# Plain gate-up sets with tokens as rows, and a higher rank for readings, sums, softmax and normalisation, in a decoder layer on one Trainium2 core

## The chip, the cores and the metric

The kernel runs on one core of a Trainium2 chip, as one launch. The time is that of the whole kernel on the device, in microseconds; it stands beside a median of three runs. The engines are named as in the profile: PE (TensorE, matmuls), PEld (its weight loads), DVE (VectorE), ACT (ScalarE), POOL (GpSimd) and SP (SyncE, which here issues most of the loads).

## The reference

One layer of a decoder, for 512 tokens (T) of 2048 features (D), all in fp32. It has two token mixers side by side, joined by gates per channel, and a SwiGLU feed-forward part of width 5632 (DFF); the normalisations are scaled and shifted by vectors made from `c`.

```python
sh_a, sc_a, gt_a, sh_f, sc_f, gt_f = split(silu(c) @ w_ada + b_ada, 6)
h = rmsnorm(x, norm_mix) * (1.0 + sc_a) + sh_a
c_q, c_kv, k_pe, q_g, k_g, v_g, z, b_logit, a_logit, gate_logits = split_cols(h @ w_in)
y_a = mla_branch(c_q, c_kv, k_pe, ...) @ w_o_mla          # 8 heads, causal softmax over 512 keys
y_b = gdn_branch(conv_silu(q_g, k_g, v_g), z, b_logit, a_logit, ...) @ w_o_gdn   # gated delta rule
g_a, g_b = split(sigmoid(gate_logits), 2)
x = x + gt_a * ((g_a * y_a + g_b * y_b) @ w_o)
h = rmsnorm(x, norm_ffn) * (1.0 + sc_f) + sh_f
gate, up = split(h @ w_gate_up, 2)                         # 2 x 5632 columns
x = x + gt_f * ((silu(gate) * up) @ w_down)
return rmsnorm(x, final_norm)
```

(Written shorter than in the reference; the order and the shapes are the same.)

## The kernel before

Every fp32 operand of a matmul is split into two parts, `hi` (rounded to the matmul's format, a cast on ACT) and `lo` (the rest, a subtraction on DVE). A product is then three matmuls, hi with hi, hi with lo and lo with hi, that add up in the same bank of PSUM. Weights come by DMA and are split in the kernel: L263 is the cast to `hi`, L264 the subtraction for `lo` (`halves`); L239 and L240 do the same for activations (`hilo`).

**Units.** The work of TensorE is a list of *units*. A unit has a load (a DMA by SP), a split, a list of matmuls, and a step before and after them. For a plain weight matrix a unit is two row tiles of 128 by 512 columns. `Driver.run` takes the units in order, and keeps two of them split ahead (`AHEAD`) and up to four loaded. The parts split from weights stand in pools of four buffers each (`SPLITS`). Tiles of 128x512 for all else come from one pool of 68 (`SLOTS`). Matmuls write to 8 PSUM banks.

**Chains.** Side work (normalisation, sums, stores) is written as generators, *chains*. After every 12 matmuls counted (`GROUP`), each chain makes one step; `weight` says how much one matmul counts, and `hold` puts the next step off by 12.

**Order.** The instructions of PE, SP and POOL keep the order of the program (`PINNED`). DVE and ACT are ordered when the kernel is built, by a list scheduler: of the instructions that are ready the one with the lowest rank goes first, and the rank is the place in the program. `tc.high_priority(n)` takes n off the rank of what is issued inside it. Before the change, the work touched by it has its plain rank.

**Stages.** In order: the modulation vectors; the products with `w_in`, in sets of 512 columns; the delta rule and the attention in between; the two output products (`ya`, `yb`); the product with `w_o`, three quarters of it by a form of Strassen's method (`strassen`) and the last quarter, `wo3`, in two halves of 256 tokens (`half_sets`); the feed-forward part; its down product with the last normalisation.

**Around the change.** `wo_half_done` reads the banks of a half of `wo3`: it adds the gated result to the stream x2 (L1432), squares it on ACT, and adds up the squares (L1444). `part_rstd` sums the squares over the features with matmuls into a bank (`hss`), computes the reciprocal root with a row of small operations on DVE (`token_rstd`, `rsqrt`, L229 to L233 and L417) and makes a diagonal tile of it (L1467); `spread` broadcasts it over the rows with one matmul (`hbc`). `h2_gen` is the chain that then normalises the eight groups `q` of a token half `h` (two row tiles of 256 tokens each, L1752 and L1753), and splits each group for the matmuls. The chain of the first half starts in the second half of `wo3`, that of the second half in `gu0`.

The gate-up product takes 11 sets of 512 inner columns. The last ten (`big(1)` to `big(10)`) go by Strassen's method with tokens as the rows of the result; what they produce is turned by PE transposes in the second half of the set that follows (`turned_a`, which reads `turning`) and stored to `f_dram`, from where the down product reads it. The first 512 inner columns are two plain sets, `gu0` and `gu1`, of 256 gate and 256 up columns each: here the weights stand still and 256 tokens move, in two halves, so that the result has features as rows and needs no turning. `gu0` goes over all weights for one half of the tokens, then over all of them for the other half; `gu1` takes both halves with each weight tile. `gu_done` reads the banks at the end of a set: Silu of the gate on ACT, times the up part on DVE, stored from the tile `sl`.

`done` is the step that reads the banks of a set in general (`fm_set` for features as rows, `tm_set` for tokens as rows), `after` the same in the Strassen sets; `softmax`, `transposes` and `values` are the steps of the attention.

Of the kernel before, what the change touches and what calls it, by code (L numbers as in the profile page):

```python
# [11 lines left out]
AF = mybir.ActivationFunctionType  # L12
# [7 lines left out]
KT = 16  # L20
# [9 lines left out]
AHEAD = 2  # L30
LOADS = 4
GROUP = 12


class Unit:
# [136 lines left out]
def block_kernel(ctx: ExitStack, tc: tile.TileContext, a: dict, out, out_t):  # L172
# [34 lines left out]
    def tok(j):  # L207
        return slice(j * P, (j + 1) * P)

    def h4(ap):  # L210
        return ap.rearrange("p (h d) -> p h d", h=4)

# [67 lines left out]
    def fm_set(name, loads, width, kt, x, done, ks=None, lo_eng=None, st=None, small=False, cols=slice(0, T), alone=False, late=False,  # L280
               in_parts=()):
        widths = [min(P, width - o) for o in range(0, width, P)]
        st = {} if st is None else st

        def unit(k0, nk):
            box = {}

            def start():
                box["raw"] = fetch(loads(k0, nk), width, nk, small)

            def split():
                box["w"] = halves(box.pop("raw"), width, nk, nc.gpsimd if lo_eng and k0 % 4 == 0 else None, small)

            if in_parts and k0 == 0:
                def start():
                    raw = box["raw"] = raws.tile([P, nk, width], F32, tag="raw", name=nm("raw"))
                    for dst, src in loads(k0, nk):
                        for cs in in_parts:
                            load(dst(raw)[:, :, cs], src[:, :, cs])

                def split(between):
                    raw = box.pop("raw")
                    hi = his.tile([P, nk, width], F32R, tag="hi", name=nm("hi"))
                    lo = los.tile([P, nk, width], F32R, tag="lo", name=nm("lo"))
                    box["w"] = hi, lo
                    for i, cs in enumerate(in_parts):
                        nc.scalar.copy(hi[:, :, cs], raw[:, :, cs])
                        if i == 0:
                            between[0]()
                        nc.vector.tensor_tensor(lo[:, :, cs], raw[:, :, cs], hi[:, :, cs].bitcast(F32), ALU.subtract)  # L310
                        if i == 0:
                            between[1]()

            def pre():
                if k0 == 0 and cols.start == 0:
# [12 lines left out]

            def post():
                if k0 + nk == kt and done is not None:  # L330
                    done(st["ps"])
                    drv.hold()

            return Unit(start, split, mms, pre, post, alone=alone, late=late and k0 + nk == kt)

        return [unit(k0, nk) for k0, nk in ks or [(k, 2) for k in range(0, kt, 2)]]

    def tm_set(name, loads, kt, x, done, nk=2, ts=tuple(range(NT)), lo_eng=None, weight=1, alone=False, xt=None):
# [5 lines left out]
        def unit(k0):  # L344
# [21 lines left out]

            def post():
                if k0 + nk == kt:
                    done(st["ps"])
                    drv.hold()  # L370

            return Unit(start, split, mms, pre, post, weight=weight, alone=alone)
# [789 lines left out]
    def attention():  # L1162
# [5 lines left out]
        def scores(i):  # L1168
# [8 lines left out]
            if qb == 3:  # L1177
                del QN[h], KN[h], qpT[h]
                if h == 7:
                    kpT.clear()  # L1180

        def softmax(i):
            h, qb = items[i]
            N = (qb + 1) * P
# [8 lines left out]
            nc.vector.tensor_scalar(p[:, 0:N], p[:, 0:N], r, None, op0=ALU.mult)  # L1193
            box[i]["p"] = p

        def transposes(i):
            h, qb = items[i]
            N = (qb + 1) * P
            p = box[i].pop("p")
            ps = PS("pT")  # L1200
            for kb in range(qb + 1):
                nc.tensor.transpose(ps[:, tok(kb)], p[:, tok(kb)], ident)
            s = S("pT")
            (nc.scalar.copy if i % 2 else nc.vector.tensor_copy)(s[:, 0:N], ps[:, 0:N])
            box[i]["pT"] = s

        def values(i):
            h, qb = items[i]
            s = box[i].pop("pT")
# [228 lines left out]
    def squares(q, seg, eng):  # L1438
# [6 lines left out]
        else:  # L1445
            st.append(s)

    def part_rstd(segs):

        ps = PS("hss")  # L1450
# [37 lines left out]
    def half_sets(name, loads, x, done):  # L1488
# [3 lines left out]
        def unit(h, k0):  # L1492
# [20 lines left out]

            def post():
                if k0 + 2 == KT:
                    done(h, st[h])
                    st[h] = None
                    drv.hold()

# [220 lines left out]
    def start_h2(h):  # L1740
        return lambda: h2c.append(drv.add(h2_gen(h)))

    def h2_gen(h):

        yield 3 if h else 1
# [1 line left out]
        yield 6 if h else 4  # L1747
        r = spread(*diag)
        for q in range(8):
            f = S("h2f")  # L1750
            for k in (2 * q, 2 * q + 1):
                nc.vector.scalar_tensor_tensor(half_of(f, k), half_of(x2[h][q], k), s_ffn[:, k:k + 1], r, op0=ALU.mult, op1=ALU.mult)  # L1752
                nc.scalar.activation(half_of(f, k), half_of(f, k), AF.Identity, bias=sh_ffn[:, k:k + 1])  # L1753
            x2[h][q] = None
            h2f[h][q] = f
            h2T[h][q] = hilo(f[:], "h2")
            h2n[h] = 2 * q + 2
            yield 2

    w_gu, w_dn = a["w_gate_up"][0], a["w_down"][0]  # L1760
# [38 lines left out]
    def big(s):  # L1799
# [64 lines left out]
        def tt(o, x, y):  # L1864
            nc.vector.tensor_tensor(o, x, y[:], ALU.add)  # L1865

        def after(c, t):
            if c == "m1":
                nc.scalar.copy(v[t], ps["m1"][t][:])
# [126 lines left out]
    def strassen(w, c1, c0, products, ready, outputs, freed):  # L1996
# [6 lines left out]
        def unit(k):  # L2003
# [28 lines left out]

            res = {}

            def after(c):
                def tt(name, x, y, op):
                    s_ = res[name] = euvw[0][:, "euvw".index(name), :] if name in "euvw" else S(name)[:]
# [99 lines left out]
        return lambda k0, nk: [(lambda r: r[:, :, 0:256], wrows(w_gu, k0, nk, 256 * s, 256)),  # L2137
                               (lambda r: r[:, :, 256:512], wrows(w_gu, k0, nk, DFF + 256 * s, 256))]

    def gu_done(s, ps):  # L2140

        f = {}

        def done(j, h):
            if h == 0:
                return
            for h in range(2):
                fs, v = slice(256 * (j % 2), 256 * (j % 2) + 256), ps[j][:, 256 * h:256 * h + 256]
                if j < 2:
                    if j == 0:  # L2150
                        f[h] = S("sl")
                    nc.scalar.activation(f[h][:, fs], v, AF.Silu)
                else:
                    nc.vector.tensor_tensor(f[h][:, fs], f[h][:, fs], v, ALU.mult)
                if j == 3:
                    side(f_dram[s, h], f[h][:])
        return done

    def gu_both(s):

        st = {}

        def unit(k0):
            box = {}
# [6 lines left out]

            def pre():
                if k0 == 0:
                    st["ps"] = [PS(f"gu{s}") for _ in range(4)]
                    st["done"] = gu_done(s, st["ps"])

            def after(j, h):
                st["done"](j, h)

            mms = []  # L2180
            for kk in range(2):
                k = k0 + kk
                for j in range(4):
                    for h in range(2):
                        for n, (wi, xi) in enumerate(((0, 0), (0, 1), (1, 0))):
                            mms.append(lambda kk=kk, k=k, j=j, h=h, n=n, wi=wi, xi=xi: mm(
                                st["ps"][j][:, 256 * h:256 * h + 256], box["w"][wi][:, kk, tok(j)], half_k(h2T[h][k // 2], k)[xi],
                                start=k == 0 and h == 0 and n == 0, stop=k == KT - 1 and n == 2, skip_group_check=True))
                        if k == KT - 1:
                            mms[-1] = lambda m=mms[-1], j=j, h=h: (m(), after(j, h))  # L2190

            def post():
                if k0 + 2 == KT:
                    for q in range(4):
                        h2T[1][q] = None

            return Unit(start, split, mms, pre, post, late=k0 + 2 == KT)

        return [unit(k0) for k0 in range(0, KT, 2)]

# [14 lines left out]
    xc = []  # L2215

    def ffn():
        def gu0():
            us, st = [], {}

            def done(ps):
                done_ = gu_done(0, ps)
                for j in range(4):
                    for h in range(2):
                        done_(j, h)

            for h in range(2):
                half = fm_set("gu0", gu_loads(0), 512, KT, lambda k, h=h: half_k(h2T[h][k // 2], k), done if h else None, st=st,
                              cols=slice(256 * h, 256 * h + 256), alone=True)
                for i, u in enumerate(half):  # L2230
                    def ahead(h=h, k=min(2 * i + 4, KT)):
                        while h2n[h] < k:
                            drv.step(h2c[h])
                    with_pre([u], ahead)
                us.append(half)
# [6 lines left out]
            with_pre(us[0], start)  # L2242
            return us[0] + us[1]

        def reload_a(k):
            aT[k] = S("ah", F32R), S("al", F32R)
# [186 lines left out]
                    yield  # L2433

        yield from gu0()
        yield from with_pre(gu_both(1), lambda: xc.append(drv.add(combine())))
# [92 lines left out]
```

## Time and profile before

| | before |
|---|---|
| median of 3 runs | 2735.57 us |
| lowest and highest | 2734.82, 2736.35 us |
| span of the profiled execution (its one time on the page) | 2731.7 us |
| instructions | 41089 |
| PE busy | 2705.7 us, 99% |
| DVE busy | 2098.3 us, 77% |
| ACT busy | 1204.9 us, 44% |
| mean granted clock of PE | 0.998 |

The profile is of one execution. Busy time counts an engine's own instructions; matmuls overlap, and their ends are modelled, so that the pace of a row of matmuls is better read from the distance of their starts. The list of waits says what an engine waited for, in total, how often, and the longest. The chain of waits is the work that ended last, followed back from the end; each of its lines has a start, a duration, the engine, the tile written, the line of the code, and how many instructions followed one another without a wait. A timeline has one line for an operation, with the idle time ahead of it and what ended that in brackets.

### The profile page before, as it was taken

How to read it: one execution, taken by the hardware profiler on the slowest of the kernel's cores; microseconds unless marked ns; L12 is line 12 of the kernel's file. 1: busy time of each engine (PE TensorE's matmuls, PEld its weight loads, DVE VectorE, ACT ScalarE, POOL GpSimd, SP SyncE). 2: the span in 40 equal slices, each digit the busy share in tenths (PEclk: the TensorE clock that was granted, in tenths of full speed). 3: DMA queues.
4: the chain of work that ended last, by engine and by line, in shares of the span. 5: the costliest groups of instructions: out<-in, count | busy, mean ns of one | idle time of the engine just before them, and what ended most of it. 6: DMA issues, size and time to landing. Idle time of an engine off the chain costs nothing.

```text
span 2731.7 us, 41089 instructions
## 1 busy us (share of the span) xinstructions
PE 2705.7 (99%) x15304; PEld 2351.8 (86%) x15304; DVE 2098.3 (77%) x3361; ACT 1204.9 (44%) x1717; POOL 258.8 (9%) x361
## 2 busy tenths in 40 slices
PE   9999999999999999999999999999999999999998
PEld 7888788888888888889999888888888888998997
DVE  8784656677977886788787877778787777877877
ACT  3443432442344343234473444444444446446445
POOL 0000011102101000001000000000000103113113
PEclk9999999999999999999999999999999999999999
DMA  9896455646666978725854556665655668569565
GB/s 364 302 357 215 143 177 173 190 144 185 198 187 194 315 253 313 258 78 131 268 185 136 195 201 208 204 208 198 212 190 198 214 212 208 132 194 202 126 190 178
DMA packets 315489, 562.20 MB, mean 206 GB/s; under 512 B 40772, under 2 KB 120916, under 8 KB 315288
## 3 DMA queue, kind: packets, MB, share of 16 engines
q1 hardware_dynamic: 264776, 458.99, 51.6%
q0 software_dynamic: 31872, 74.76, 10.6%
q10 hardware_dynamic: 18640, 25.83, 2.7%
q8 instruction: 120, 1.97, 0.3%
q14 instruction: 81, 0.66, 0.1%
HBM read 476.62 MB, written 83.89 MB: 205 GB/s over the span
## 4 chain that ended last, share of the span: by engine, by line
PE 90%; DVE 4%; DMA 3%; issue 2%; ACT 1%; SPq 0%; DVEq 0%; ACTq 0%; POOL 0%
PE m L155 41%; PE gb L155 6%; PE v L155 4%; PE gu L155 3%; PE z L155 3%; PE ya L155 3%; PE k L155 3%; PE q L155 3%; PE yb L155 3%; PE dn L155 3%; PE s L155 3%; PE ckv L155 2%; PE cq L155 2%; PE wo L155 1%; PE qk L155 1%
## 5 line engine op out<-in xcount | busy, mean ns | idle before, releaser
L263 ACT CAST hi<-raw 128x1024 fp32r<-128x1024 f32 x249 | 258.8, 1041 | 538.9 <-DMA raw<-in_w_in_dram 164.9
L264 DVE TENSOR_TENSOR lo<-raw,hi 128x1024 fp32r<-128x1024 f32 x249 | 302.6, 1216 | 202.4 <-ACT hi L263 197.6
L1847 ACT CAST hi<-raws 128x512 fp32r<-128x512 f32 (+1 forms) x240 | 218.6, 911 | 328.0 <-PE m L155 269.2
L1848 DVE TENSOR_TENSOR lo<-raws,hi 128x512 fp32r<-128x512 f32 (+1 forms) x240 | 247.4, 1042 | 83.9 <-ACT hi L1847 83.6
L155 PE MATMUL m<-xh,lo 128*128 128x256 f32 x1088 | 308.4, 283 | 1.3 <-DVE lo L2023 1.3
L155 PE MATMUL m<-xh,hi 128*128 128x256 f32 x1088 | 308.1, 283 | 1.5 <-ACT hi L2022 1.5
L155 PE MATMUL m<-xl,hi 128*128 128x256 f32 x1088 | 307.9, 283 | 0.0
L449 DVE CUSTOM_DVE_ANT_0 rawm<-rawm,cbc 128x1024 f32<-128x1024 f32 x192 | 232.1, 1230 | 2.0 <-DMA rawm<-in_w_mod_dram 1.7
L155 PEld LDWEIGHTS m<-xh,lo 128*128 128x128 f32 x1088 | 208.8, 192 | 2.0 <-DVE lo L2023 1.9
L155 PEld LDWEIGHTS m<-xh,hi 128*128 128x128 f32 x1088 | 208.9, 192 | 1.7 <-ACT hi L2022 1.7
L155 PEld LDWEIGHTS m<-xl,hi 128*128 128x128 f32 x1088 | 208.9, 192 | 0.1
L155 PE MATMUL m<-hi,h2h 128*128 128x512 f32 x480 | 190.1, 396 | 0.0
L155 PE MATMUL m<-hi,h2l 128*128 128x512 f32 x480 | 187.2, 390 | 0.0
L155 PE MATMUL m<-lo,h2h 128*128 128x512 f32 x480 | 187.2, 390 | 0.0
L2022 ACT CAST hi<-sums 128x1024 fp32r<-128x1024 f32 x88 | 92.2, 1048 | 134.4 <-PE m L155 102.4
L2023 DVE TENSOR_TENSOR lo<-sums,hi 128x1024 fp32r<-128x1024 f32 x88 | 107.4, 1220 | 45.5 <-ACT hi L2022 45.4
L1847 ACT CAST hi<-sums 128x1024 fp32r<-128x1024 f32 x80 | 84.2, 1053 | 109.4 <-PE m L155 104.5
L1848 DVE TENSOR_TENSOR lo<-sums,hi 128x1024 fp32r<-128x1024 f32 x80 | 97.6, 1220 | 26.7 <-ACT hi L1847 26.1
L155 PEld LDWEIGHTS m<-hi,h2l 128*128 128x128 f32 x480 | 90.1, 188 | 19.0
L155 PEld LDWEIGHTS m<-hi,h2h 128*128 128x128 f32 x480 | 90.2, 188 | 18.5 <-DVE euvw L1865 0.7
L155 PEld LDWEIGHTS m<-lo,h2h 128*128 128x128 f32 x480 | 90.3, 188 | 17.5
L2022 ACT CAST hi<-raws 128x768 fp32r<-128x768 f32 x88 | 73.4, 835 | 66.8 <-PE m L155 48.1
(581 smaller groups left out, 7418.3 us busy)
## 6 DMA issues: line engine op xcount, KB each, us to landing
raws<-in_w_gate_up_dram SPq DMA_DIRECT2D x400, 256.0 KB, 3.6
rawm<-in_w_mod_dram SPq DMA_DIRECT2D x192, 512.0 KB, 5.4
raw<-in_w_in_dram SPq DMA_DIRECT2D x143, 512.0 KB, 4.6
raws<-in_w_down_dram SPq DMA_DIRECT2D x128, 256.0 KB, 3.9
s_dram<-raws POOLq DMA_DIRECT2D x80, 256.0 KB, 2.3
raws<-s_dram SPq DMA_DIRECT2D x80, 256.0 KB, 3.3
rawa<-in_w_in_dram SPq DMA_DIRECT2D x32, 512.0 KB, 4.6
raws<-in_w_o_dram SPq DMA_DIRECT2D x48, 256.0 KB, 3.1
```

Of the source, the lines that this page charges most:

```text
L155: return self.tc.keep_in_program_order(f(*args, **kwargs))
L263: nc.scalar.copy(hi[:], raw[:])
L264: (lo_eng or nc.vector).tensor_tensor(lo[:], raw[:], hi[:].bitcast(F32), ALU.subtract)
L449: r = nc.vector.tensor_tensor_reduce(raw, raw, c, 1.0, 0.0, ALU.mult, ALU.add, parts[:, k, half:half + 1])
L1847: nc.scalar.copy(hi[:], src)
L1848: nc.vector.tensor_tensor(lo[:], src, hi[:].bitcast(F32), ALU.subtract)
L2022: nc.scalar.copy(hi[:], src)
L2023: nc.vector.tensor_tensor(lo[:], src, hi[:].bitcast(F32), ALU.subtract)
```

## The change

It has two parts. First, `gu0` and `gu1` now have tokens as the rows of the result (`gu_tokens`): 128 tokens of the normalised input stand still and 512 weight columns (256 gate, 256 up) move. `gu0` still takes one half of the tokens after the other. Each matmul counts double for the chains. `gu_read` reads a bank as soon as it is complete, into one of four tiles (`first_tiles`) that both sets fill; after `gu1` these are handed to `turned_a`, which turns them with PE in the second half of `big(1)`, copies them on ACT and stores them. The stores from `sl` are gone.

Second, `soon` gives what is issued in it a rank that is 600 lower: the bank readings `done` of `fm_set`, `tm_set` and `half_sets`, the steps `softmax`, `transposes` and `values` of the attention, the sums of squares with the reciprocal root (`part_rstd`), the readings `after` of the Strassen sets, and the normalisation of one group, which is now a function of its own (`normalize`).

```diff
+SOON = 600
...
+    def soon(f):
+        def g(*args, **kwargs):
+            with tc.high_priority(SOON):
+                return f(*args, **kwargs)
+        return g
...
             def post():        # fm_set, tm_set and, with (h, st[h]), half_sets
                 if k0 + nk == kt and done is not None:
-                    done(st["ps"])
+                    soon(done)(st["ps"])
                     drv.hold()
...
+        @soon
         def softmax(i):        # also transposes, values, part_rstd, and after in big and strassen
...
+    @soon
+    def normalize(h, q, r):
+        f = S("h2f")
+        for k in (2 * q, 2 * q + 1):
+            nc.vector.scalar_tensor_tensor(half_of(f, k), half_of(x2[h][q], k), s_ffn[:, k:k + 1], r, op0=ALU.mult, op1=ALU.mult)
+            nc.scalar.activation(half_of(f, k), half_of(f, k), AF.Identity, bias=sh_ffn[:, k:k + 1])
+        x2[h][q] = None
+        h2f[h][q] = f
+        h2T[h][q] = hilo(f[:], "h2")
+        h2n[h] = 2 * q + 2
...
     def h2_gen(h):
...
         for q in range(8):
-            f = S("h2f")
...
+            normalize(h, q, r)
             yield 2
...
-    def gu_done(s, ps):
...
-    def gu_both(s):
...
+    first_tiles = {}
+
+    def gu_read(s, ht, bank):
+        if s == 0:
+            first_tiles[ht] = S("g0")
+        o, g = first_tiles[ht][:, 256 * s:256 * s + 256], S("sl")
+        nc.scalar.activation(g[:, 0:256], bank[:, 0:256], AF.Silu)
+        nc.vector.tensor_tensor(o, g[:, 0:256], bank[:, 256:512], ALU.mult)
+
+    def gu_tokens(s, hts):
...
+            def one(kk, h, t, n, xi, wi):
                 k = k0 + kk
+                mm(banks[h, t][:], half_k(h2T[h][k // 2], k)[xi][:, tok(t)], box["w"][wi][:, kk, :],
+                   start=k == 0 and n == 0, stop=k == KT - 1 and n == 2)
+                if k == KT - 1 and n == 2:
+                    gu_read(s, (h, t), banks.pop((h, t)))
...
             def post():
-                if k0 + 2 == KT:
+                if k0 + 2 == KT and s == 1:
                     for q in range(4):
                         h2T[1][q] = None
-            return Unit(start, split, mms, pre, post, late=k0 + 2 == KT)
+                    turning.append((0, first_tiles))
+            return Unit(start, split, mms, pre, post, weight=2, alone=s == 0, late=k0 + 2 == KT)
```

More of the change, by code (lines that the diff above doesn't have):

```diff
@@ L368, in post @@
                 if k0 + nk == kt:
-                    done(st["ps"])
+                    soon(done)(st["ps"])
                     drv.hold()
@@ L1205, in transposes @@
             box[i]["pT"] = s
+        @soon
         def values(i):
@@ L1446, in squares @@
             st.append(s)
+    @soon
     def part_rstd(segs):
@@ L1515, in post @@
                 if k0 + 2 == KT:
-                    done(h, st[h])
+                    soon(done)(h, st[h])
                     st[h] = None
@@ L1741, in start_h2 @@
         return lambda: h2c.append(drv.add(h2_gen(h)))
+    @soon
+    def normalize(h, q, r):
[7 more added lines that the diff above has]
+        h2n[h] = 2 * q + 2
     def h2_gen(h):
@@ L1749, in h2_gen @@
         for q in range(8):
-            f = S("h2f")
[L1751 to L1757, printed above, removed]
+            normalize(h, q, r)
             yield 2
@@ L1865, in tt @@
             nc.vector.tensor_tensor(o, x, y[:], ALU.add)
+        @soon
         def after(c, t):
@@ L2033, in unit @@
             res = {}
+            @soon
             def after(c):
@@ L2138, in gu_loads @@
                                (lambda r: r[:, :, 256:512], wrows(w_gu, k0, nk, DFF + 256 * s, 256))]
-    def gu_done(s, ps):
[L2142 to L2157, printed above, removed]
-    def gu_both(s):
-        st = {}
+    first_tiles = {}
[6 more added lines that the diff above has]
+    def gu_tokens(s, hts):
+        banks = {}
         def unit(k0):
@@ L2173, in pre @@
                 if k0 == 0:
[L2174 to L2181, printed above, removed]
-                k = k0 + kk
[L2183 to L2190, printed above, removed]
+                    for ht in hts:
+                        banks[ht] = PS(f"gu{s}")
+            def one(kk, h, t, n, xi, wi):
+                k = k0 + kk
+                mm(banks[h, t][:], half_k(h2T[h][k // 2], k)[xi][:, tok(t)], box["w"][wi][:, kk, :],
+                   start=k == 0 and n == 0, stop=k == KT - 1 and n == 2)
+                if k == KT - 1 and n == 2:
+                    gu_read(s, (h, t), banks.pop((h, t)))
+            mms = [lambda kk=kk, h=h, t=t, n=n, xi=xi, wi=wi: one(kk, h, t, n, xi, wi)
+                   for kk in range(2) for h, t in hts for n, (xi, wi) in enumerate(((0, 0), (0, 1), (1, 0)))]
             def post():
-                if k0 + 2 == KT:
+                if k0 + 2 == KT and s == 1:
                     for q in range(4):
                         h2T[1][q] = None
-            return Unit(start, split, mms, pre, post, late=k0 + 2 == KT)
+                    turning.append((0, first_tiles))
+            return Unit(start, split, mms, pre, post, weight=2, alone=s == 0, late=k0 + 2 == KT)
         return [unit(k0) for k0 in range(0, KT, 2)]
@@ L2218, in gu0 @@
         def gu0():
[L2219 to L2225, printed above, removed]
+            us = []
             for h in range(2):
-                half = fm_set("gu0", gu_loads(0), 512, KT, lambda k, h=h: half_k(h2T[h][k // 2], k), done if h else None, st=st,
-                              cols=slice(256 * h, 256 * h + 256), alone=True)
+                half = gu_tokens(0, [(h, t) for t in range(2)])
                 for i, u in enumerate(half):
@@ L2234, in gu0 @@
                     with_pre([u], ahead)
-                us.append(half)
+                us += half
             def start():
@@ L2241, in start @@
                 start_h2(1)()
-            with_pre(us[0], start)
-            return us[0] + us[1]
+            with_pre(us, start)
+            return us
         def reload_a(k):
@@ L2435, in ffn @@
         yield from gu0()
-        yield from with_pre(gu_both(1), lambda: xc.append(drv.add(combine())))
+        both = gu_tokens(1, [(h, t) for h in range(2) for t in range(2)])
+        yield from with_pre(both, lambda: xc.append(drv.add(combine())))
         side(g_dram.rearrange("(k p) -> p k", p=P), gt_ffn[:])
```

## The prediction

> **What bounds the kernel now.** I read the page first, for which engine sets the pace, then the waits of TensorE, then the chain of waits, then busy time by stretches around the edited sets, and last the timelines of DVE and ACT there.
>
> ```profile
> span 2731.7 us, 41089 instructions
> PE 2705.7 (99%) x15304; PEld 2351.8 (86%) x15304; DVE 2098.3 (77%) x3361; ACT 1204.9 (44%) x1717; POOL 258.8 (9%) x361
> ```
>
> TensorE is busy for 99% of the span, so the time is the pace of its matmuls plus the few places where it stands. The other engines matter only where they let it stand. DVE, at 77%, is the one that can. The waits of TensorE, most of them:
>
> ```profile
> PE hss L155 <- DVE sq L1444: 2.2, 1, 2.2
> PE dn L155 <- DVE g L2038: 1.7, 1, 1.7
> PE ga L155 <- DVE lo L264: 1.7, 3, 1.0
> PE cq L155 <- ACT sz L962: 0.9, 1, 0.9
> PE sc L155 <- ACT P L1191: 0.7, 1, 0.7
> PE yT L155 <- DVE pT L1204: 0.5, 1, 0.5
> ```
>
> Columns: total us, times, longest. Five of these (hss, dn, cq, sc, yT, 6.0 us together) wait for work that the change moves ahead; ga waits for a split of weights (line 264), which the change moves behind other work. All of it is small, so the change can win little by removing waits and could lose as much by making new ones. The profiled span stands 3.9 us below the median of the runs, 2735.57 us. My sum is made against 2731.7, and 3.9 is added at the end. I take 0.2%, 5.5 us, as about what a measurement of this kernel can tell from no change.
>
> **Matmuls of the two plain sets.** Both forms have rows in the chain of waits (start, us, engine, operation, count):
>
> ```profile
> 234.12 43.52 PE k L155 x192
> ...
> 1397.04 76.31 PE gu L155 x636
> ...
> 1601.68 4.12 PE m L155 x18
> 1606.23 4.12 PE m L155 x18
> ```
>
> A gu matmul of 256 columns comes every 76.31/636 = 0.1200 us, a k matmul of 512 columns every 43.52/192 = 0.2267. The sets gu0 and gu1 have 3 x 256 = 768 matmuls of 256 columns:
>
> ```profile
> L155 PE MATMUL gu<-h2h,hi 128*128 128x256 f32 x256 | 72.7, 284 | 0.0
> L155 PE MATMUL aT<-kc,g 128*128 128x128 f32 x160 | 23.9, 272 | 0.0
> ...
> 1426.00:1473.00 47.00, 47.00 (x394) 47.00 (x393) 36.53 (x51) 19.96 (x33) 3.34 (x5) 1.00 0.45 124
> ```
>
> The last line is the stretch of gu1: us, busy time of PE, PEld, DVE, ACT and POOL with instructions, then granted clock, DMA share, GB/s.
>
> Before: 768 x 0.1200 = 92.2 us. After: 384 x 0.2267 = 87.1. That is **-5.1**: one matmul of 512 is 13 ns cheaper than two of 256. By the Trainium skill's "TensorE: Matmul & The Clock Gate", section "Back-to-back issue gap", an isolated matmul takes N/2.4 + 2.5 ns, 109 and 216 here, so the sets would go from 83.8 to 82.9 and gain only 0.9, which speaks against the change; the rows show 120 and 227, and the measurement decides.
>
> Counted double, 384 matmuls advance the chains of side work as 768 did, so these stay in place per column. Each bank is now read by one Silu and one multiply of 256 columns, 16 operations per set as before. In gu1 the banks finish 3 x 0.2267 = 0.68 us apart, before 6 x 0.12 = 0.72, so the next product gets its banks no later: nothing, covered by a DVE with 10 us free in that stretch.
>
> The token-major result has to be turned: 16 transposes more on TensorE (aT goes from 160 to 176), four at a time inside the second half of the first Strassen set, as later sets do it. The two m rows lie 1606.23 - 1601.68 - 4.12 = 0.43 us apart, which is four such transposes: 4 x 0.43 = **+1.7**. The four copies on ACT and four stores that go with them replace two pairs of stores between the sets; TensorE waits for neither. POOL loses the stores that its next one, of sums of weights, was queued behind. Four more tiles live until then; by the lives of the tiles in the trace at most 61 of 68 are taken there, so no load waits for one. Sets: **-3.4**.
>
> **The wait for the sums of squares.** DVE before it, and the stretches around it, with gu0's and that of the dn stall:
>
> ```profile
> 1355.65 0.47 DVE L1432 SCALAR_TENSOR_TENSOR x<-wo,gt_mix,x 128x256 f32<-128x256 f32 x1
> 1356.04 1.21 DVE L264 TENSOR_TENSOR lo<-raw,hi 128x1024 fp32r<-128x1024 f32 x1
> 1357.17 0.68 DVE L1444 TENSOR_TENSOR sq<-sq,sq 128x512 f32<-128x512 f32 x1
> ...
> 1355.40:1359.20 3.80, 1.55 (x12) 1.38 (x11) 3.59 (x5) 0.63 (x1) 0.00 (x0) 0.92 0.35 115
> 1359.20:1362.20 3.00, 3.00 (x16) 3.00 (x16) 1.53 (x4) 0.29 (x1) 0.00 (x0) 0.53 0.78 267
> 1380.00:1426.00 46.00, 46.00 (x384) 45.95 (x384) 40.13 (x71) 35.39 (x55) 0.00 (x0) 1.00 0.60 190
> ...
> 2455.00:2463.00 8.00, 6.29 (x47) 5.65 (x45) 7.93 (x12) 5.67 (x10) 0.00 (x0) 1.00 0.77 269
> ```
>
> DVE is full here (3.59 of 3.80), and one split, 1.13 us from start to start, lies ahead of the last sum. With rank the readings and the sums go first, the split behind them; the two stores that ACT issues in the reading go ahead with it, and nothing is queued on them. The stall falls by that 1.1, not by 2.2. After it TensorE ran at 0.53 of its clock for 3 us: 16 matmuls that take 1.9 at full pace, 1.1 lost. The dn stall of 1.7 lies in the last stretch at 1.00, so a stall of 1.1 should cost no clock. Together **-2.2**. By the section "Part 1: The HAM clock gate" of the same page of the Trainium skill, half rate follows an idle window of about 3.4 us, and stalls under that would cost no clock here; the row shows that 2.2 was enough.
>
> **The other waits.** In the dn stall DVE has splits in front of the reading:
>
> ```profile
> 2458.55 1.88 DVE L240 TENSOR_TENSOR xl<-a,xh 128x512 fp32r<-128x512 f32 x3
> 2460.47 0.69 DVE L2123 TENSOR_TENSOR a<-a,a 128x512 f32<-128x512 f32 x1
> 2461.08 1.22 DVE L264 TENSOR_TENSOR lo<-raw,hi 128x1024 fp32r<-128x1024 f32 x1
> 2462.22 0.68 DVE L2038 TENSOR_TENSOR g<-euvw,m 128x512 f32<-128x512 f32 x1
> ```
>
> Rank puts g in front, and nothing behind it is due within the stall. dn, cq, sc and yT are 3.8 us; I take **-3.0**, since the cq wait is for a bank read by ACT whose own chain may be late. Readings elsewhere push splits back by a few operations; ga waits 1.7 for splits already. I bound this by 0 and +3 and take 0: most sets have few readings per set, and TensorE stands nowhere else for a split of L264.
>
> **The normalisation.** This is the large unknown. For each of two token halves, eight groups of two row tiles are normalised: the first half in the second part of wo3, the other in gu0. The timelines of DVE and ACT in gu0 show how they lie now:
>
> ```profile
> 1401.53 0.87 DVE L1752 SCALAR_TENSOR_TENSOR h2f<-x,s_ffn,hbc 128x256 f32<-128x256 f32 x2
> 1402.34 1.23 DVE L264 TENSOR_TENSOR lo<-raw,hi 128x1024 fp32r<-128x1024 f32 x1
> 1403.80 0.69 DVE L240 TENSOR_TENSOR h2l<-h2f,h2h 128x512 fp32r<-128x512 f32 x1 [0.23 <-ACT h2h L239]
> 1404.41 0.87 DVE L1752 SCALAR_TENSOR_TENSOR h2f<-x,s_ffn,hbc 128x256 f32<-128x256 f32 x2
> ...
> 1402.21 0.90 ACT L1753 ACTIVATE h2f<-h2f,sh_ffn 128x256 f32<-128x256 f32 x2
> 1403.15 0.62 ACT L239 CAST h2h<-h2f 128x512 fp32r<-128x512 f32 x1
> 1404.14 1.05 ACT L263 CAST hi<-raw 128x1024 fp32r<-128x1024 f32 x1 [0.37 <-PE gu L155]
> ```
>
> One group, then one split, in turn, each in the 2.88 us (24 x 0.12) of a unit. A group takes DVE 0.81 + 0.61 = 1.4 us and ACT 0.94 + about 0.5 = 1.4. All eight become ready at once, when the broadcast reciprocal (hbc) lands; 600 ranks cover the whole of them (a unit is some 24 instructions of TensorE and a few others, and a group is emitted about every unit), so all eight may go ahead of every split: 8 x 1.4 = 11.4 us during which ACT casts no weights. The cover is the buffers of split weights. ACT's cast waits for TensorE ("<-PE gu"), so all four buffers are full, and a cast starts three units before its need: 3 x 2.72 (a unit of 12 x 0.2267) = 8.2 us, less cast and subtraction 1.05 + 1.23 = 2.3, is 5.9 us. In wo3, with units still of 2.88, it is 6.4. So each burst stalls TensorE by between 0 (splits slip into gaps, or the eight are not all ready) and 11.4 - 5.9 = 5.5 us, plus 1.1 of slow clock where it passes about 2.2. I take the middle of the stall, 2.8, and the clock, 3.9 a burst: **+7.8** for two.
>
> Sum: -3.4 - 2.2 - 3.0 + 7.8 = -0.8. 2731.7 - 0.8 + 3.9 = **2734.8 us**.
>
> **Rivals.** *Faster: the bursts stay hidden.* DVE has 46.0 - 40.1 = 5.9 us free in gu0 and ACT 10.6; the whole work fits, if splits get into the gaps. For: in the rows above the ready group alternates with a split. Against: they alternate because order by program position makes them, and the change replaces that. Then -3.4 - 2.2 - 3.0 = -8.6, which is 2727.0.
>
> *Slower: both bursts hold the splits in full,* in the wo3 half and at the start of gu0. They start behind work that is itself moved ahead: the reciprocal's ten small operations, now spread between splits, and the split pushed behind the sums.
>
> ```profile
> 1364.14 0.15 DVE L232 SCALAR_TENSOR_TENSOR rs<-rs,rs 128x2 f32<-128x2 f32 x1
> 1364.33 0.16 DVE L233 SCALAR_TENSOR_TENSOR rs<-rs,rs 128x2 f32<-128x2 f32 x1
> ```
>
> So the first burst finds its splits late by another 1.1 and the reciprocal's about 2.5 (an estimate: some twelve, with the diagonal, at the 0.19 between these). The price: 5.0 + 1.1 + 3.6 and 5.5 + 1.1 = 16.3, against -6.4 from the sets and the other waits, the gain at hss being lost in it: +9.9, 2745.5. It decides from about 4.3 us a burst, where it eats the 8.6; from 7.1 a burst on, the kernel is measurably slower.
>
> *The change doesn't do what it says:* the pace goes by columns alone, and 512 cost two of 256. Then -5.1 is 0 and the time 2739.9. Against it stand 192 matmuls in a row at 0.2267; for it only that these have other operands.
>
> **How the numbers follow.** My forecast (bursts half hidden) and what lies near it, 2730 to 2741, gets 0.38, the third rival within it 0.03; the first rival 0.31, with the mild cases between; the second 0.28. The range takes in the first rival with the 0.8 more that the other waits may give, and the second in full: 2726 to 2746. Alone, the forecast's own range is 2730 to 2741. Faster by over 0.2% is 0.31, within it 0.41, slower 0.28.
>
> **What the profile after would show.** Right: gu groups with 512 columns, 3 x 128 of them, at 0.227 apart, the two sets in 87 us and not 92; aT 176 times; the waits of dn, cq, sc, yT gone, and hss at about 1.1; in DVE's timeline behind hbc, a run of sixteen L1752 with hardly an L264 among them, and TensorE waiting for lo L264 or hi L263 by 2 to 5 us twice, near 1375 and near 1405, with a granted clock below 1 after it. Wrong: no such waits (the first rival), waits over 6 us (the second), or a gu pace of 0.24. Waits for lo in the attention stage or between q, k and v would show that the readings cost what I took as nothing.

## The result and the profile after

The changed kernel takes 2746.16 us (median of four runs, 2743.89 to 2746.22), the kernel before 2735.36 in the runs beside it: a ratio of 1.0041 with a 95% interval of 1.0029 to 1.0053, so 11 us slower. That is 0.16 us outside the stated range (2726 to 2746), and the forecast, 2734.8, was a time 0.8 us shorter than before. Run again on another chip (f1 below), the same kernel came to 1.0045 (1.0033 to 1.0058).

The page of the kernel after, its first lines:

```profile
span 2744.4 us, 40334 instructions
...
PE 2708.6 (99%) x14936; PEld 2335.8 (85%) x14936; DVE 2098.9 (76%) x3361; ACT 1206.8 (44%) x1721; POOL 259.6 (9%) x361
```

The work is the same, and the waits of TensorE have changed. A selection of those after (us in total, times, longest):

```profile
PE m L156 <- DVE lo L2040: 5.8, 6, 3.1
PE hss L156 <- DVE sq L1455: 3.2, 1, 3.2
PE hbc L156 <- DVE diag L1479: 2.3, 1, 2.3
PE gu L156 <- ACT h2h L247: 1.7, 1, 1.7
PE cq L156 <- ACT sz L970: 0.9, 1, 0.9
PE gu L156 <- DVE h2l L248: 0.6, 1, 0.6
PE dn L156 <- DVE g L2056: 0.4, 1, 0.4
PE yT L156 <- DVE pT L1214: 0.2, 1, 0.2
```

dn, yT and sc (gone) fell, as forecast; cq did not. But hss rose from 2.2 to 3.2, and three larger waits are new: 3.1 for a split in the Strassen part of `w_o`, 2.3 at hbc, 2.3 in gu (1.7 and 0.6). Where the time went is read from the chain of waits, whose rows of TensorE begin at the borders of the stages. First the kernel before, then the kernel after:

```profile
1207.44 120.95 PE m L155 x1008
1328.40 20.05 PE wo L155 x167
...
1379.88 7.20 PE gu L155 x60
...
1473.35 127.90 PE m L155 x564
...
2252.52 16.33 PE dn L155 x72
```

```profile
1205.92 75.49 PE m L156 x629
...
1332.66 22.33 PE wo L156 x186
...
1386.58 6.83 PE gu L156 x30
...
1481.40 51.73 PE m L156 x228
...
2264.17 16.33 PE dn L156 x72
```

| stage | before | after | difference |
|---|---|---|---|
| up to the Strassen part of `w_o` | 1207.4 | 1205.9 | -1.5 |
| that part (m) | 121.0 | 126.7 | +5.8 |
| wo3 | 51.5 | 53.9 | +2.4 |
| gu0 and gu1 | 93.5 | 94.8 | +1.4 |
| ten Strassen gate-up sets | 779.2 | 782.8 | +3.6 |
| the rest, to the end of the span | 479.2 | 480.2 | +1.1 |

The differences add up to 12.7 us, where the medians differ by 10.8: each column is one execution, and single executions of the kernel before lay between 2731.2 and 2741.4 us in the later runs. So a stage's difference of one or two us is not read as the change's work unless other runs repeat it.

The largest loss lies in a stage that begins 180 us ahead of the token-major sets, and of which the diff changes only the rank of the readings at its end. The POOL engine's timeline shows why. The first two lines are of the kernel before, the other three of the kernel after:

```profile
1428.50 1.08 POOL L155 DMA_DIRECT2D f_dram<-sl  x2 [122.70 <-DVE sl L2154]
1429.57 1.18 POOL L155 DMA_DIRECT2D g_dram<-gt_ffn  x1
...
1303.83 0.54 POOL L156 DMA_DIRECT2D x<-x_dram  x1
1304.36 1.19 POOL L156 DMA_DIRECT2D g_dram<-gt_ffn  x1
1464.47 0.56 POOL L156 DMA_DIRECT2D s_dram<-raws  x1 [158.92 <-DVE raws L1842]
```

POOL keeps the order of the program. In the kernel before, the store of the gate vector (g_dram, L2437) stood behind the two stores from `sl`, and POOL waited 122.70 us for these. The change takes them away; only loads of `x` are left ahead of the store, its vector has long been there, and it goes at 1304.36 instead of 1429.57. By its access pattern, `(k p) -> p k`, neighbours in a partition lie 512 bytes apart in `g_dram`, so it writes 2048 values of 4 bytes, each for itself. What it meets there, in the DMA issues, the stretches and DVE's timeline of the kernel after:

```profile
g_dram<-gt_ffn POOLq DMA_DIRECT2D x1, 8.0 KB, 13.4
...
1310.00:1315.00 5.00, 5.00 (x44) 5.00 (x43) 0.00 (x0) 1.05 (x1) 0.00 (x0) 1.00 1.09 71
1315.00:1320.00 5.00, 2.03 (x17) 1.83 (x16) 1.95 (x4) 0.83 (x1) 0.00 (x0) 0.89 0.13 23
1320.00:1325.00 5.00, 4.91 (x23) 4.92 (x24) 3.70 (x6) 2.09 (x2) 0.00 (x0) 0.50 0.73 196
...
1318.01 0.69 DVE L2031 TENSOR_TENSOR sums<-raws 128x512 f32<-128x512 f32 x1 [9.03 <-DMA raws<-in_w_o_dram]
```

The 8 KB take 13.4 us to land. Meanwhile the DMA engines are all busy (1.09) and move 71 GB/s. DVE stands 9.03 us for the weights of `w_o`, TensorE then 3.1 us, and after that it runs at half its clock for 5 us (0.50, 23 matmuls, where the undisturbed stretch has 44).

### The profile page after: what moved, and what is told of

Same layout as the page of the kernel before. It is cut to its first block, busy times and chain, and to the rows that moved or that the text cites. A ratio compares the mean times of both kernels' runs of the same rounds, so it can differ in the third digit from the quotient of the medians.

```text
span 2744.4 us, 40334 instructions
## 1 busy us (share of the span) xinstructions
PE 2708.6 (99%) x14936; PEld 2335.8 (85%) x14936; DVE 2098.9 (76%) x3361; ACT 1206.8 (44%) x1721; POOL 259.6 (9%) x361
## 2 busy tenths in 40 slices
DMA packets 315486, 562.16 MB, mean 205 GB/s; under 512 B 40772, under 2 KB 120916, under 8 KB 315288
## 4 chain that ended last, share of the span: by engine, by line
PE 86%; DVE 6%; DMA 5%; issue 2%; ACT 1%; SPq 0%; DVEq 0%; ACTq 0%; POOLq 0%
PE m L156 40%; PE gb L156 5%; PE v L156 4%; PE z L156 3%; PE k L156 3%; PE q L156 3%; PE yb L156 3%; PE dn L156 3%; PE s L156 3%; PE gu L156 3%; PE ga L156 2%; PE ckv L156 2%; PE wo L156 2%; PE cq L156 2%; PE qk L156 1%
```

## The experiments

All ratios are to the kernel before, on the same chip, with 95% intervals; one per mille is 2.7 us. The first two runs move the one store, in the kernel after to the start of the Strassen set `big(2)`, and in the kernel before ahead of gu0's stores:

```diff
-        side(g_dram.rearrange("(k p) -> p k", p=P), gt_ffn[:])
...
+                if (s, i) == (2, 0):        # e1, in the kernel after
+                    with_pre([u], lambda: side(g_dram.rearrange("(k p) -> p k", p=P), gt_ffn[:]))
...
+                side(g_dram.rearrange("(k p) -> p k", p=P), gt_ffn[:])    # e2, in the kernel before: start() of gu0
                 start_h2(1)()
```

> The kernel after, with the one store of the gate vector (g_dram, 8 KB) issued by POOL at the start of the Strassen set big(2) instead of between gu1 and big(1). In the kernel after, POOL issues this store at 1304 us, because the stores from sl that stood ahead of it in POOL's order are gone; the weight load of w_o that follows takes 14.4 us and TensorE stands 3.1 us at 1317. Theory 1 (the store blocks the load): the stall and the slow clock behind it go, 5.8 us, so about 2740.4. Theory 2 (the rank of the readings in the Strassen part of w_o brings the splits late): nothing changes there, 2746.

> The kernel before, with the same store put ahead of gu0's stores in POOL's order, so that it goes as soon as its vector is there; nothing else changes. Theory 1 (the store blocks the load): TensorE gets a stall of about 3 us near 1318 and a slow clock behind it, 2735.4 + 5.8 = about 2741. Theory 2 (rank): 2735.4, no stall.

e1: 1.0058 (1.0044 to 1.0071), no better than the kernel after, so the forecast of 2740.4 failed. Yet the stall at 1317 is gone, the `w_o` part takes the 121.0 us of the kernel before again, and the same store makes a larger stall in the new place:

```profile
g_dram<-gt_ffn POOLq DMA_DIRECT2D x1, 8.0 KB, 15.4
...
PE m L156 <- DVE lo L1864: 5.0, 1, 5.0
```

So the store costs by what it collides with; the choice of place was bad, the theory of the stall held. e2: 1.0017 (1.0009 to 1.0026). This one move, with the sets and the ranks as before, makes the kernel before 4.7 us slower, about as forecast. In its profile the store takes 14.3 us to land, but the wait in the `w_o` part is 1.1 and not 3, and that part is only 1.4 us longer; hss waits 3.7 instead of 2.2, and wo3 is 3.0 us longer.

The next two do one half of the change each: the token-major sets with plain rank (`soon` returns `f` as it is), and the rank with the old sets.

> The kernel after with plain rank everywhere: only the token-major sets, and with them the store at 1304. Theory A (the losses come with the token-major sets: the early store 5.8, and the readings of two banks in the middle of gu0, which with a table load take ACT and DVE where they are needed): the stall at 1317 stays, stalls in gu0 stay, and the time is 2743 to 2747. Theory B (the losses come from rank, the sets win their 3.4): 2732 without the stall at 1317, 2738 if only the store costs.

> The kernel before with the rank alone: the sets stay feature-major, the store stays behind the stores from sl. Theory A (the losses come with the sets): no stall at 1317, the stages up to 1029 are 2.2 us shorter and the dn stall 1.3, so 2731 to 2733. Theory B (the losses come from rank): 2746 plus the 3.4 that the sets win, about 2749, with the stalls at 1317, at hss and in gu0.

e3: 1.0033 (1.0021 to 1.0046), with a wait of 3.0 at 1317 and waits in gu0 (2.6 for h2h, 1.5 at hbc). e4: 1.0001 (0.9992 to 1.0010), with none of these. The loss comes with the sets; theory B falls. But the rank wins nothing that shows either: in e4's profile the waits at sc and yT are gone (1.2 us) and dn's is 0.9 shorter, but hss waits 3.2 here too, where e3 has 2.3, a wait of 1.8 at ya is new, and the first Strassen sets of the down product lose 0.8.

The next four runs put back, one on another, what the change moved. The store's source becomes a copy that can only be made after gu0's banks are read; then the two banks of gu0's first half are read at its end; then hbc comes one step of the chain later; then the rank stays only in the attention and in `after`.

```diff
+        gh = S("gh")                                                   # e5 to e8, f2, g2
+        nc.vector.scalar_tensor_tensor(gh[:, 0:16], first_tiles[1, 1][:, 0:16], 0.0, gt_ffn[:], op0=ALU.mult, op1=ALU.add)
-        side(g_dram.rearrange("(k p) -> p k", p=P), gt_ffn[:])
+        side(g_dram.rearrange("(k p) -> p k", p=P), gh[:, 0:16])
...
-                    gu_read(s, (h, t), banks.pop((h, t)))
+                    waiting.append((s, (h, t), banks.pop((h, t))))      # e6, e7, e8, g2
+                    if s == 1 or h == 1:
+                        for w in waiting:
+                            gu_read(*w)
+                        waiting.clear()
...
-        yield 6 if h else 4
+        yield 7 if h else 4                                            # e7, e8, g2
```

> The kernel after, with the store of the gate vector fed from a copy that DVE can make only after gu0's banks are read, so that POOL issues it near 1440 us, about where the kernel before had it. Theory 1 (the store costs by what it collides with: 5.8 in w_o, more in the Strassen sets, nothing between gu0 and gu1): no stall at 1317, none of over 1.5 us in the Strassen sets, 5.8 less than the kernel after, a ratio to before of 1.002 (about +5). Rival (the store costs the same wherever it is put): ratio 1.004 to 1.006.

> As the run with the held store, and the two banks of the first token half of gu0 are read at the end of gu0, as in the kernel before, not in its middle. Theory (the reading, with its table load, puts DVE's and ACT's normalisation of the second half behind it): the waits of gu for h2h and h2l, 2.3 us, and the slow clock behind them go, 2.5 to 3.5 less than the run with the held store. Rival (the normalisation is late because hbc is late): the waits stay.

> As the run that reads late, and the broadcast hbc of the second half is put one more step of the chain later, 6 matmuls or 1.4 us. Theory (the chain of small operations takes as long as before, but TensorE, with shorter units, is at hbc sooner): the wait at hbc falls from 2.3 to about 1 us and its slow clock goes, 1.5 to 2.5 less. Rival (what is gained at hbc is lost again, since the normalisation starts as late): no change, with a wait for h2h or h2l in the second half.

> As the run with hbc later, with the higher rank kept only in the attention steps and the readings after of the Strassen sets; the readings done, the sums of squares with the reciprocal, and the normalisation have plain rank again. Theory (the rank of done makes the in-order DVE and ACT stand at a reading whose matmuls are not done, which holds up the squares): the wait at hss goes back from 3.2 to 2.2, while the gains at dn (1.3) and in the attention (1.0) stay; 1 to 1.5 less than the run with hbc later. Rival (rank does not decide at hss): no change.

e5: 1.0039 (1.0026 to 1.0053). The stall at 1317 was gone from its profile, but the time was not 1.002, so this alone did not settle the store. e6: 1.0013 (1.0004 to 1.0022); the waits of gu for h2h and h2l are gone and the two sets are 3.8 us shorter than in e5. e7: 1.0006 (0.9997 to 1.0015): the wait at hbc fell to 1.0, but the sets as a whole did not get shorter. From hbc on, e6 had a matmul every 72.09/318 = 0.2267 us and e7 every 72.58/312 = 0.2326, so the rival holds in the profile as far as the loss goes: the units wait a little each. That hbc's place alone makes these waits is not shown; g2 below has the same place without them. In the times e6 and e7 cannot be told apart.

```profile
1400.53 72.09 PE gu L156 x318
...
1400.77 72.58 PE gu L156 x312
```

e8: 1.0005 (0.9996 to 1.0014), the same as e7 within the intervals and not the 1 to 1.5 us less that was expected; its wait at hss is 2.2 again, as the theory had it, which is worth too little to be told in the whole.

Since e5 and the kernel after had run on different chips, both were run on one, with two more: the store in the order of its partitions, `(p k) -> p k`, 128 pieces of 64 bytes, at the early place (the gates then stand in another order; the work is the same); and a version in which only gu1 is token-major, gu0 and its stores are those of before, and the rank is that of e8.

> The kernel after, unchanged, beside the next three on one chip: 1.004 of before, with the stall at 1317.

> The kernel of the run with the held store again, beside the kernel after on one chip. Theory 1 (the early store is the larger part of the loss): 4 to 6 us less than the kernel after. Rival (the 5.8 us that the profile shows at 1317 come back elsewhere, or are of that one execution): as the kernel after.

> The kernel after with the store of the gate vector at the same place, but written in the order of its partitions: 128 pieces of 64 bytes instead of 2048 of 4 (the vector then stands in another order, so that the last gate is wrong; everything else is the same work). Theory (the number of pieces makes the store block the queues): no stall at 1317, and the time of the held store, 4 to 6 us less than the kernel after. Rival (any store at that place delays the load): the stall stays.

> A version for the best time: gu0 as in the kernel before (features as rows, its stores ahead of the gate vector's), only gu1 with tokens as rows and its 8 transposes, and the higher rank only in the attention steps and the readings after of the Strassen sets. The sum of what the runs showed: gu1 192 x 0.2267 against 384 x 0.1200, -2.6; 8 transposes, +0.9; attention -1.0, dn -0.9, the other Strassen sets of the down product +0.8: -2.8, or 0.999 of before. Rival (the transposes and stores of the first Strassen set cost more there than the set wins): 1.000 to 1.001.

The kernel after: 1.0045 (1.0033 to 1.0058). The store held: 1.0022 (1.0013 to 1.0030), 6 us less. In 128 pieces: 1.0025 (1.0014 to 1.0035), as good as held, at the early place; its landing and the stretch where the kernel after moved 71 GB/s:

```profile
g_dram<-gt_ffn POOLq DMA_DIRECT2D x1, 8.0 KB, 6.4
...
1310.00:1315.00 5.00, 5.00 (x44) 5.00 (x43) 3.04 (x6) 1.85 (x3) 0.00 (x0) 1.00 0.30 112
1315.00:1320.00 5.00, 5.00 (x45) 5.00 (x43) 2.52 (x3) 1.85 (x2) 0.00 (x0) 1.00 0.88 249
```

The same bytes in longer pieces take 6.4 us; DVE stands 1.93 us for the weights there, as in the kernel before (2.06), and TensorE does not wait. It is the number of pieces, and with it their length. The Trainium skill says on the page "DMA: Bandwidth & Descriptors", section "Rules for kernel authors", that a last dimension that is not contiguous becomes one descriptor for each element; the run agrees in the time, 13.4 us against 6.4. The profile's count of DMA packets does not show the pieces: it is 315486 in the kernel after and 315470 here, 16 less. On this chip the store is half of the 12 us; with the other measurement of the held kernel, 1.0039 on another chip, it would be under 2, so in the whole time its share stands at 2 to 6 us. In the stage itself it is clear of such noise. The `w_o` part takes 121.0 us in all thirteen profiles in which no store in 2048 pieces meets it. In the kernel after, e3 and f1, where one does, it takes 126.7, 125.7 and 125.0, each with the stall (3.1, 3.0 and 2.3 us): 4 to 6 us more. gu1 alone token-major (f4): 0.9996 (0.9987 to 1.0005), no change that shows, though the 0.999 of its sum lies in the interval.

What was left was hss. The first and the third run start its sums two steps of the chain later for the first half (`yield 3` for `yield 3 if h else 1`), on the version with gu1 alone and on the kernel before; the second takes the rank of wo3's reading from e7 (`done(h, st[h])`).

> The version with only gu1 token-major, and the sums of squares of the first half (hss, on TensorE) two steps of the chain later, 24 matmuls or 2.9 us. Theory (hss is early for DVE, and the normalisation behind it has about 8 us to spare): the wait of 2.3 and the 1.1 of slow clock go, 3 us less than that version, 0.9985 of before. Rival (the normalisation comes late instead): waits of gu for h2h or h2l, no gain.

> The version with the held store, the late reading and hbc later, with one thing taken from the higher rank: the reading done of the two halves of wo3. Theory (its rank alone sets the wait at hss): 2.2 instead of 3.2. Rival (the rank of part_rstd or of the normalisation does it): 3.2 stays.

> The kernel before, with hss of the first half two steps later as in the first run of this call. Theory: 3 us less than before, 0.9989. Rival: no change.

g1: 0.9998 (0.9989 to 1.0007), which excludes the 0.9985 of its theory. g3: 0.9992 (0.9984 to 1.0001), which holds both its theory's 0.9989 and no change. In g3's profile wo3 is 2.7 us shorter, the slow clock gone, and gu0 and gu1 2.4 longer:

```profile
PE gu L155 <- DVE h2l L240: 1.1, 5, 0.3
PE hss L155 <- DVE sq L1444: 1.0, 1, 1.0
```

What hss no longer waits, gu waits for the normalisation that starts later; g1's profile has the same waits. g2: 0.9995 (0.9986 to 1.0004). hss waits 2.6, between 3.2 and the 2.2 of e8, so the reading's rank is a part of it and not all. From hbc on, its matmuls come every 70.77/312 = 0.2268 us, without e7's small waits; in its profile gu0 and gu1 together are 4.3 us shorter than before.

```profile
1397.86 70.77 PE gu L156 x312
```

No version was shown to beat the kernel before; the best two, g3 and g2, have intervals that hold 1.

## Why the prediction was wrong

**The step that failed first: the stores on POOL.** The prediction saw that "POOL loses the stores that its next one, of sums of weights, was queued behind", and costed it at nothing. The next one was not that, it was the store of the gate vector, at 1429.57, and it moved by 125 us into loads that were needed. This is the 5.8 us of the `w_o` part (4.1 in f1). No rival had it. The slower rival came out at 2745.5, close to what was measured, but by another mechanism, the bursts, so its number is a coincidence. It is luck as well that the forecast missed by no more than 11 us: its +7.8 for the bursts did not come, and without them its sum is the -8.6 of the first rival, 19 us from the measured +10.8.

**The reading of the banks.** "Each bank is now read by one Silu and one multiply ... nothing" was worked out for gu1 only (the 16 operations are those of both sets, 8 in each). In gu0 the first half's banks are now read in its middle, and not at its end. ACT's and DVE's timelines of the kernel after:

```profile
1414.95 1.28 ACT L2165 ACT_TABLE_LOAD   x1
1416.24 0.39 ACT L2165 ACTIVATE sl<-gu 128x256 f32<-128x256 f32 x1
...
1412.86 0.87 DVE L1759 SCALAR_TENSOR_TENSOR h2f<-x,s_ffn,hbc 128x256 f32<-128x256 f32 x2
...
1416.66 0.42 DVE L2166 TENSOR_TENSOR g<-sl,gu 128x256 f32<-128x256 f32 x1 [1.01 <-ACT sl L2165]
1417.60 1.23 DVE L272 TENSOR_TENSOR lo<-raw,hi 128x1024 fp32r<-128x1024 f32 x1 [0.52 <-DMA raw<-in_w_gate_up_dram]
...
1419.07 0.86 DVE L1759 SCALAR_TENSOR_TENSOR h2f<-x,s_ffn,hbc 128x256 f32<-128x256 f32 x2
```

The table load holds ACT for 1.28 us, DVE stands 1.01 at the multiply that waits for it, and the next group of the normalisation, due 2.7 us after 1412.86, starts at 1419.07. That is the wait of 1.7 and 0.6 in gu. e6, which reads these banks late, shows it: the two waits are gone, gu0 and gu1 are 3.8 us shorter in the profile, and the ratio is 0.0026 below e5's (0.0009 below f2's, which is the kernel of e5 on another chip). How much of it is the table load and how much the reading itself was not separated.

**The bursts did not come.** The +7.8 rested on all eight groups going ahead of the splits. They alternate with the splits as before:

```profile
1381.01 0.87 DVE L1759 SCALAR_TENSOR_TENSOR h2f<-x,s_ffn,hbc 128x256 f32<-128x256 f32 x2
1381.82 1.23 DVE L272 TENSOR_TENSOR lo<-raw,hi 128x1024 fp32r<-128x1024 f32 x1
1383.28 0.69 DVE L248 TENSOR_TENSOR h2l<-h2f,h2h 128x512 fp32r<-128x512 f32 x1 [0.23 <-ACT h2h L247]
1383.88 0.86 DVE L1759 SCALAR_TENSOR_TENSOR h2f<-x,s_ffn,hbc 128x256 f32<-128x256 f32 x2
```

The prediction had named the sign to look for ("a run of sixteen L1752"), and it was absent. e4 puts the price of the rank in gu0 and gu1 at 0.6 us. Why the order stays is not shown; the order is fixed when the kernel is built, and no run tried what the scheduler could choose from. A wait in the same stretch came in another way: with the units shorter, TensorE came to hbc before the diagonal was made, and waited 2.3 (0.3 in e4, with the units of before).

**hss went the other way.** Forecast -2.2, measured +2.4 in wo3: the wait is 1.0 longer, and the rest goes with a longer stretch of slow clock behind it. That stretch differs from run to run: e4, with the same wait of 3.2, has only +0.8 in wo3. DVE's timeline of the kernel after, then ACT's of after and of before:

```profile
1355.02 1.66 DVE L1443 SCALAR_TENSOR_TENSOR x<-wo,gt_mix,x 128x256 f32<-128x256 f32 x4 [1.44 <-PE wo L156]
1356.60 0.68 DVE L248 TENSOR_TENSOR a21l<-a,a21h 128x512 fp32r<-128x512 f32 x1
1357.20 2.35 DVE L272 TENSOR_TENSOR lo<-raw,hi 128x1024 fp32r<-128x1024 f32 x2
1359.47 0.68 DVE L1455 TENSOR_TENSOR sq<-sq,sq 128x512 f32<-128x512 f32 x1
...
1357.33 3.22 ACT L1453 ACTIVATE sq<-x 128x512 f32<-128x512 f32 x6
...
1350.74 2.19 ACT L1442 ACTIVATE sq<-x 128x512 f32<-128x512 f32 x4
```

The rank puts the four readings first in DVE's order. DVE is in order, so it stands 1.44 us until TensorE has finished the bank, with a21l and two splits, which it could have done, behind. On ACT the squares of the other tiles, which before ran at 1350.74, ahead of the reading, now come behind it at 1357.33. "The split behind them" was the whole argument; that the reading was not ready when its turn came was not asked. The rank makes it, and not the sets: 2.3 with the sets alone (e3), 3.2 with the rank alone (e4). Taking all rank from this place gives 2.2 again (e8), from the reading alone 2.6 (g2).

**What held.** The pace: 0.2268 us where nothing waits (g2), against 0.2267; the -5.1 is there, but hidden by waits until the store, the reading, hbc and the rank of wo3's reading are put right, and then 4.3 of it. The transposes are 176, and the ten Strassen sets, +3.6, hold their 1.7 and waits that differ from run to run (the stage is 2.2 to 4.8 longer in the versions with both token-major sets, e1 aside, 0.5 with the rank alone, and 1.8 in g3, which changes neither; what is the sets' beyond the 1.7 is open). The waits at sc and yT fell by 1.0 and at dn by 1.3, against 3.0 forecast for these and cq. Only the 0.7 at sc is shown to be the rank's: it is there in all four profiles with plain rank and in none of the others. yT and dn show no wait in g3, with plain rank, and dn waits 1.7 in e1, f3 and g1, with the reading's rank raised.

## What to carry to other kernels

When an instruction leaves an in-order queue, look up by name what stood behind it and when that will now go: a store whose data are ready moves up to the end of what is left ahead of it, and can land in the middle of loads that count. A higher rank in an order that is fixed at build time is no preference at run time; if its data come late, the engine stands with ready work behind it. A gain on an engine that is 99% busy shows only if the engines that feed it, here at 87% and 77% in gu0, can keep the new pace.

## What was not expected of the hardware

A store of 8 KB in 2048 pieces took 13.4 to 15.4 us to land where it met loads without room to spare, and cost TensorE waits of 1.1 (e2) to 5.0 us (e1) there; in 128 pieces it took 6.4, and the time was that of the held store. To land late is not the cost by itself: held, the 2048 pieces still took 10.8 (f2) and 11.7 us (e5), and TensorE did not wait there. And the length of a wait does not tell whether the clock falls. The stretches of the kernel after behind hss, from hbc on and behind the wait in gu, then, in the last line, behind the same wait in f2:

```profile
1363.10:1368.00 4.90, 4.76 (x22) 4.79 (x23) 2.64 (x6) 0.33 (x1) 0.00 (x0) 0.52 0.36 122
...
1405.00:1420.00 15.00, 15.00 (x67) 12.42 (x68) 11.44 (x19) 12.58 (x21) 0.00 (x0) 1.00 0.44 137
1422.20:1427.20 5.00, 4.39 (x18) 3.29 (x19) 3.54 (x8) 2.62 (x5) 0.00 (x0) 1.00 0.68 213
...
1417.10:1422.10 5.00, 4.39 (x12) 3.19 (x13) 3.50 (x7) 1.52 (x3) 0.00 (x0) 0.69 0.68 213
```

Behind the 3.2 us at hss TensorE ran at 0.52 for about 5 us, behind the 2.3 at hbc at 1.00, and behind the 2.2 at hss in the kernel before at 0.53. One and the same wait shows it best: the 1.7 us for h2h in gu is followed by a clock of 1.00 in the kernel after, e5 and f1, and by 0.69 over the 5 us behind it in f2, 0.67 in e1 and 0.73 in f3. The Trainium skill, page "TensorE: Matmul & The Clock Gate", section "Part 1: The HAM clock gate", says that the window in which activity is watched runs free; that fits these waits, but where the window lay was not measured in any run here.
